# First pieces of x in 256 columns ahead of their weights, and square sums by a column of ones, in a hybrid decoder layer on one core

## The chip, the cores and the metric

The kernel runs on one core of one Trainium2 chip. The metric is the device time of one execution in microseconds (us); the median of several runs counts. The engines are TensorE (PE, with its weight loads as PEld), VectorE (DVE), ScalarE (ACT), GpSimd (POOL) and SyncE (SP), which here only issues loads and stores.

## What is computed

A decoder layer for 256 tokens of width 2048, all in float32. The input x is normed per row and goes through one combined projection to 12304 columns. Two mixers read its parts. Branch A is a gated DeltaNet with 8 heads of 128: queries, keys and values pass a causal convolution of four taps and a SiLU, and then a chunked delta rule. Branch B is a block attention with 8 heads of 128, which for 256 tokens is plain causal attention. Both are gated, projected, merged with sigmoid gates, projected once more, normed, and added to x. What matters for the change, cut from the reference:

```python
def l2_normalize(x):
    return x * lax.rsqrt(jnp.sum(x * x, axis=-1, keepdims=True) + NORM_EPS)
...
    h = rms_norm(x, pre_norm_w[l])
    proj = h @ w_in
...
    qkv = jax.nn.silu(causal_depthwise_conv(gdn_qkv, conv_w)).astype(jnp.float32)
    qa, ka, va = jnp.split(qkv, 3, axis=-1)
    qa, ka, va = l2_normalize(to_heads(qa)), l2_normalize(to_heads(ka)), to_heads(va)
```

So each head of the queries needs the sum of the squares of its 128 elements, per token.

## The kernel before, in words

**Products in parts.** Every large projection is done in two parts of float32r: an operand is cast to `hi` by ACT and the rest `lo` is the operand less `hi`, by DVE. A product is hi by hi, hi by lo and lo by hi, summed in PSUM. `split` (L220) does this for weights, in tiles of three buffers each, ahead of PE. Weights come through SP's queue into `raw`, by `proj_t` (L340), which has the weights stationary and gives channels by tokens, loading rows of 256 columns, and `proj_n` (L358), which has the activations stationary and gives tokens by channels, loading rows of 512 columns. `mm` (L146) and `tr` (L149) record matmuls and transposes, so PE's instructions have the line L147 or L150; both keep program order on PE.

**The start.** All loads of the start are issued by SP in the order of the code (L160 to L172): first the norm's weights `nrow`, then four times the pattern "512 columns of x, as two tiles of 128 tokens (L170), then four tiles of 128 rows by 512 columns of the keys' weights (L172)". PE waits with products of ones (`warm`), turns `nrow` into a column per 128 channels (`pnc`, L293; DVE copies it to `ncol`), and then turns x: `turn(c)` (L237) transposes the four tiles of 128 channels of one piece, eight transposes into `hTp`. `turned` (L248) writes the scaled result as hi (ACT, for k=1 DVE) and lo (DVE, L256) into `hT`. `first_split` (L274) casts the keys' weights (L278, L279), and `first_products` (L282) does the four heads' products of one k, eight instructions. The loop at L302 takes for each piece the products of its first two k, turns the next piece, takes the squares of x for the norm (`stats`), and then the products of its last two k. The reciprocal norm is applied later, since it is a factor per row.

**Ticks.** The work beside the projections hangs in queues of generators (`Queue`, L47). After every six or eight large products a `tick` lowers each queue's wait by 0.5; when it reaches zero the next part is put into the program there, and it says how long to wait for the part after. So PE's order is fixed by the code and by constants such as `SC_WAIT` and `A_WAIT1`. The order of the blocks of projections is the list `ORDER` (L42): queries 0 and 1 early, `kq2` and `kq3` (keys and queries of a pair of heads) later, the attention's `mk0` to `mk3` behind them, then gates and the branch pairs.

**Queries and scores.** `queries` projects two heads, convolves them and queues `score_pair` (L504). It writes hi and lo of keys and queries side by side into `kq` (ACT L509, DVE L510), and after `SC_WAIT` calls `scores` (L524) for each head. That makes two PSUM tiles `s1` and `s2` (both shown as `s`) of keys by keys and keys by queries, six products (L529), then two transposes of the queries' tile into the free half of `s2` (L532). DVE takes the diagonal of keys by keys for the keys' square sums (L534, L537). ACT squares the transposed queries and sums along the row, once for each 128 tokens (L542, `jq`), into `ssq`. `ssq` is used much later, in `normed` (L910). DVE scales the scores into `gdn` (L547, L555).

**Attention.** `attend` (L1031) waits `A_WAIT1`, does the scores `ms` of one head (L1034, L1035), the mask and the maximum on DVE, the exponentials on ACT; after `A_WAIT2` three transposes `pp`, after `A_WAIT3` the products `po` with the values, which DVE gates into `zm` (L1062). `turned_attention` (L1065) transposes `zm` (`pt`) after `A_WAIT4`. Two queues hold the heads of even and odd number. The keys `y_mk` of a pair are scaled by the row norm on DVE (L1084) before the scores. `branch_pair` (L832) empties these queues before its own products start. While the outputs of branch A are turned, `held` stops them.

Of the kernel before, what the change touches and what calls it, by code (L numbers as in the profile page):

```python
# [10 lines left out]
BF16 = mybir.dt.bfloat16  # L11
AF = mybir.ActivationFunctionType
# [3 lines left out]
P = 128  # L16
# [15 lines left out]
V_WAIT = 8  # L32
SV_WAIT = 1
OS_WAIT = 3
A_WAIT1 = 1.5
A_WAIT2 = 3
A_WAIT3 = 2
A_WAIT4 = 4
# [36 lines left out]
def hybrid_layer(  # L75
# [15 lines left out]
    nc = tc.nc  # L91
    B, S, D = x.shape
    NT = S // P
# [6 lines left out]
    xf = x.rearrange("b s d -> (b s) d")  # L100
# [15 lines left out]
    wk = ctx.enter_context(tc.tile_pool(name="wk", bufs=2))  # L116
# [7 lines left out]
    def acc_tile(name):  # L124
        return acc.tile([P, 512], F32, tag="acc", name=name)

    def aux_tile(name):
        return aux.tile([P, 512], F32, tag="aux", name=name)
# [17 lines left out]
    def mm(*args, **kwargs):  # L146
        return pin(nc.tensor.matmul(*args, **kwargs))  # L147

    def tr(*args):  # L149
        return pin(nc.tensor.transpose(*args))  # L150
# [8 lines left out]

    NCH = KT // 4  # L160
    nrow = cst.tile([KT, P], F32, name="nrow")
    nc.sync.dma_start(nrow, pre_norm_w.rearrange("o (k p) -> (o k) p", p=P))
    prow = big.tile([P, P], F32, tag="ga", name="prow")
    xall = big.tile([P, NT, D], F32, tag="u1", name="x")
    xs = [xall[:, t, :] for t in range(NT)]
    rawk = [big.tile([P, KT // 2, 512], F32, tag=f"g{i}", name=f"rawf_k{i}") for i in range(2)]
    for c in range(NCH):
        for t in range(NT):
            cs = slice(c * 512, (c + 1) * 512)
            nc.sync.dma_start(xs[t][:, cs], xf[t * P : (t + 1) * P, cs])  # L170
        for k in range(4 * c, 4 * c + 4):
            nc.sync.dma_start(rawk[k // 8][:, k % 8], w_in[k * P : (k + 1) * P, CK : CK + 512])  # L172


    ones = cst.tile([P, P], F32, name="ones")
    nc.vector.memset(ones, 1.0)
    ident = cst.tile([P, P], F32, name="ident")
# [56 lines left out]
    ssx = cst.tile([P, NT, 4], F32, name="ssx")  # L234
    pfirst = [acc_tile(f"a_k0_{m}") for m in range(4)]

    def turn(c):  # L237

        pts = []
        for k in range(4 * c, 4 * c + 4):  # L240
            if k % 2 == 0:
                pt = aux_tile(f"hTp_{k}")
            pts.append((k, pt[:, k % 2 * S : (k % 2 + 1) * S]))
            for t in range(NT):
                tr(pts[-1][1][:, t * P : (t + 1) * P], xs[t][:, k * P : (k + 1) * P], ident)
        return pts

    def turned(pts):  # L248
        for k, pr in pts:
            if k == 1:  # L250
                pin(nc.vector.tensor_scalar_mul(hT[:, k, :S], pr, ncol[:, k : k + 1]))
            else:
                pin(nc.scalar.activation(hT[:, k, :S], pr, AF.Copy, scale=ncol[:, k : k + 1]))
        for k, pr in pts:
            pin(
                nc.vector.scalar_tensor_tensor(  # L256
                    hT[:, k, S:], pr, ncol[:, k : k + 1], hT[:, k, :S].bitcast(F32), op0=ALU.mult, op1=ALU.subtract
                )
            )
# [14 lines left out]
    def first_split(k, n):  # L274
        hi = wspl.tile([P, 2, 512], F32R, tag="hi", name=f"hi_k0_{k}")
        lo = wspl.tile([P, 2, 512], F32R, tag="lo", name=f"lo_k0_{k}")
        raw = rawk[k // 8][:, k % 8 : k % 8 + n]
        pin(nc.scalar.copy(hi[:, :n], raw))  # L278
        pin(nc.vector.tensor_tensor(lo[:, :n], raw, hi[:, :n].bitcast(F32), op=ALU.subtract))  # L279
        return [(k + i, hi[:, i], lo[:, i]) for i in range(n)]  # L280

    def first_products(parts):  # L282
        for k, hi, lo in parts:
            for part in range(2):
                for m in range(4):
                    ms, pt = slice(m * P, (m + 1) * P), pfirst[m]
                    if part == 0:
                        mm(pt, hi[:, ms], hT[:, k, :], start=(k == 0), stop=False)
                    else:
                        mm(pt[:, :S], lo[:, ms], hT[:, k, :S], start=False, stop=(k == KT - 1))  # L290

    pnc = aux_tile("pnc")
    tr(pnc[:, :KT], nrow, ident[:KT, :KT])  # L293
    pin(nc.vector.tensor_copy(ncol, pnc[:, :KT]))
    pts = turn(0)
    for i in range(WARM2):
        mm(warm[:, :P], ones, ones, start=True, stop=True)
    turned(pts[:2])
    parts = first_split(0, 1) + first_split(1, 1)
    turned(pts[2:])  # L300
    parts += first_split(2, 2)
    for c in range(NCH):  # L302
        first_products(parts[4 * c : 4 * c + 2])
        if c + 1 < NCH:
            turned(turn(c + 1))
        if c == 0:
            parts += first_split(4, 2)
        stats(c)
        first_products(parts[4 * c + 2 : 4 * c + 4])
        for k in (4 * c + 6, 4 * c + 8):  # L310
            if k < KT:
                parts += first_split(k, 2)
# [174 lines left out]
    def sl(h):  # L487
        return gsl[h // HG][:, h % HG, :]
# [5 lines left out]
    ssk, ssq = nrm[:, 0], nrm[:, 1]  # L494
# [9 lines left out]
    def score_pair(h, kT, qT):  # L504
        kqs = []
        for m in range(2):
            kq = big.tile([P, 2, 2 * S], F32R, tag=("tt", "tw")[m], name=f"kq_{h + m}")
            for i, y in enumerate((kT[m], qT[m])):
                nc.scalar.copy(kq[:, i, :S], y)  # L509
                nc.vector.tensor_tensor(kq[:, i, S:], y, kq[:, i, :S].bitcast(F32), op=ALU.subtract)  # L510
            kqs.append(kq)
        yield SC_WAIT
        for m in range(2):
            yield from scores(h + m, kqs[m], qT[m])

        for b in range(4):
            t, p_ = b // 2, b % 2
            c0 = t * 4 * P + p_ * 64
            nc.gpsimd.dma_start(
                l_d[b, h : h + 2].rearrange("h j i -> j h i"),  # L520
                gsl[h // HG][p_ * 64 : p_ * 64 + 64, h % HG : h % HG + 2, c0 : c0 + 64],
            )

    def scores(h, kq, qT):  # L524
        p1 = aux_tile(f"s1_{h}")
        p2 = aux_tile(f"s2_{h}")
        for t, pt in enumerate((p1.rearrange("p (a n) -> p a n", a=2), p2[:, :S].rearrange("p (a n) -> p a n", a=2))):
            for i, (a, b) in enumerate(((0, 0), (0, S), (S, 0))):
                mm(pt, kq[:, 0, a + t * P : a + (t + 1) * P], kq[:, :, b + t * P : b + S], start=(i == 0), stop=(i == 2))  # L529
        yield 0.5  # L530
        for t in range(NT):
            tr(p2[:, (2 + t) * P : (3 + t) * P], qT[:, t * P : (t + 1) * P], ident)  # L532
        jk = wk.tile([P, P], BF16, tag="jk", name=f"jk_{h}")
        nc.vector.scalar_tensor_tensor(  # L534
            jk, p1[:, :P], 1.0, ident, op0=ALU.mult, op1=ALU.mult, accum_out=ssk[:, 0, h : h + 1]
        )
        nc.vector.scalar_tensor_tensor(  # L537
            jk, p2[:, :P], 1.0, ident, op0=ALU.mult, op1=ALU.mult, accum_out=ssk[:, 1, h : h + 1]
        )
        for t in range(NT):  # L540
            jq = wk.tile([P, P], BF16, tag="jq", name=f"jq_{h}_{t}")
            nc.scalar.activation(jq, p2[:, (2 + t) * P : (3 + t) * P], AF.Square, accum_out=ssq[:, t, h : h + 1])  # L542
        c_ = cj[:, :, h : h + 1]
        nc.vector.tensor_scalar_add(c_, ssk[:, :, h : h + 1], EPS)
        nc.vector.reciprocal(c_, c_)
        nc.vector.tensor_tensor(c_, c_, beta[:, :, h : h + 1], op=ALU.mult)
        nc.vector.scalar_tensor_tensor(  # L547
            sl(h)[:, 0 : 4 * P].rearrange("p (a n) -> p a n", a=2),
            p1.rearrange("p (a n) -> p a n", a=2),
            cj[:, 0, h : h + 1],  # L550
            dec[:, h, 0 : 2 * P].unsqueeze(1).to_broadcast([P, 2, 2 * P]),
            op0=ALU.mult,
            op1=ALU.mult,
        )
        nc.vector.scalar_tensor_tensor(  # L555
            sl(h)[:, 4 * P :].rearrange("p (a n) -> p a n", a=2),
            p2[:, : 2 * P].rearrange("p (a n) -> p a n", a=2),
            cj[:, 1, h : h + 1],
            dec[:, h, 2 * P :].unsqueeze(1).to_broadcast([P, 2, P]),
            op0=ALU.mult,  # L560
            op1=ALU.mult,
        )
        sc_left[0] -= 1
        if not sc_left[0]:
            nc.scalar.activation(sk, ssk, AF.Sqrt, bias=epst)
        yield 1
# [464 lines left out]
    def attend(h, qT, kT):  # L1031
        yield A_WAIT1
        ps = aux_tile(f"ms_{h}")
# [78 lines left out]
    for blk in ORDER:  # L1112
        n, c = blk[:2].rstrip("0123456789"), int(blk[-1])
# [126 lines left out]
    parts = []  # L1240
# [20 lines left out]
    c = 3  # L1261
    pts = [acc_tile(f"a_y{c}_{t}") for t in range(NT)]
# [43 lines left out]
```

## Time and profile before

| | us |
|---|---|
| median of three runs | 778.01 (776.86 to 778.92) |
| profiled execution | 777.05 |
| its span, first to last instruction | 775.4 |
| PE busy | 763.5 |
| DVE busy | 565.2 |
| ACT busy | 436.1 |
| POOL busy | 33.5 |

The profile is of one execution. A row of a timeline has its start in us from the span's start, its duration in us, the engine, the line, the operation, the tile written `<-` the tiles read, the shapes, and how many instructions are merged into the row (x8); in brackets stands how long the engine was idle before it and what ended that. Matmuls are pipelined: the durations of neighbours overlap, so what one costs is read from the distance of the starts. A float32 matmul shows as two instructions, a transpose or a float32r matmul as one. A row of a window has, behind its bounds and its length, the busy time and the count of each engine, the granted clock of TensorE (1.00 is full), the DMA share and GB/s. A row of waits has us in total, times, and the longest. A row of a tile has the shortest, median and longest duration in ns, and the first and last start. A row of loads has the count, the size of each, and the median us from issue to landing.

### The profile page before, as it was taken

How to read it: one execution, taken by the hardware profiler on the slowest of the kernel's cores; microseconds unless marked ns; L12 is line 12 of the kernel's file. 1: busy time of each engine (PE TensorE's matmuls, PEld its weight loads, DVE VectorE, ACT ScalarE, POOL GpSimd, SP SyncE). 2: the span in 40 equal slices, each digit the busy share in tenths (PEclk: the TensorE clock that was granted, in tenths of full speed). 3: DMA queues.
4: the chain of work that ended last, by engine and by line, in shares of the span. 5: the costliest groups of instructions: out<-in, count | busy, mean ns of one | idle time of the engine just before them, and what ended most of it. 6: DMA issues, size and time to landing. Idle time of an engine off the chain costs nothing.

```text
span 775.4 us, 10348 instructions
## 1 busy us (share of the span) xinstructions
PE 763.5 (98%) x3923; PEld 650.2 (84%) x3923; DVE 565.2 (73%) x914; ACT 436.1 (56%) x654; POOL 33.5 (4%) x61
## 2 busy tenths in 40 slices
PE   8999999999999999999999999999999999999995
PEld 7898988899888888888889888788888888888884
DVE  5777669885878898775547886686658776888853
ACT  5676666657655664454447475654455544556731
POOL 3000001112000000002001000000000000000000
PEclk9999999999999999999999999999999999999999
DMA  8576675457655556668336556657644956375912
GB/s 302 173 238 214 188 213 170 136 166 220 202 179 202 177 188 196 198 180 217 109 97 217 178 173 216 242 205 251 212 163 152 386 172 212 111 286 193 333 54 109
DMA packets 93656, 151.87 MB, mean 196 GB/s; under 512 B 3237, under 2 KB 46886, under 8 KB 93094
## 3 DMA queue, kind: packets, MB, share of 16 engines
q1 hardware_dynamic: 88902, 134.42, 53.4%
q0 software_dynamic: 4128, 15.74, 6.0%
q10 hardware_dynamic: 576, 1.05, 0.4%
q8 instruction: 31, 0.51, 0.3%
q14 instruction: 19, 0.16, 0.1%
HBM read 148.04 MB, written 3.15 MB: 195 GB/s over the span
## 4 chain that ended last, share of the span: by engine, by line
PE 95%; ACT 2%; DVE 2%; DMA 1%; SPq 0%; issue 0%; DVEq 0%
PE a_gb L147 11%; PE a_y L147 11%; PE a_ga L147 11%; PE a_zg L147 6%; PE a_mq L147 6%; PE a_v L147 6%; PE a_mk L147 6%; PE a_ub L147 6%; PE a_zm L147 6%; PE a_mv L147 5%; PE a_k L147 5%; PE a_ua L147 5%; PE a_q L147 4%; PE sv L147 2%; PE s L147 1%; DMA x<-in_x_dram 1%
## 5 line engine op out<-in xcount | busy, mean ns | idle before, releaser
L147 PE MATMUL a_ga<-hi_ga,hT 128*128 128x512 f32 x256 | 81.9, 393 | 0.0
L147 PE MATMUL a_gb<-hi_gb,hT 128*128 128x512 f32 x256 | 80.2, 390 | 0.0
L226 DVE TENSOR_TENSOR lo_gb<-raw_gb,hi_gb 128x1024 fp32r<-128x1024 f32 x32 | 38.9, 1223 | 25.1 <-ACT hi_gb L225 24.9
L147 PEld LDWEIGHTS a_gb<-hi_gb,hT 128*128 128x128 f32 x256 | 48.0, 188 | 10.6
L147 PEld LDWEIGHTS a_ga<-hi_ga,hT 128*128 128x128 f32 x256 | 48.1, 188 | 10.1
L225 ACT CAST hi_gb<-raw_gb 128x1024 fp32r<-128x1024 f32 x32 | 33.3, 1051 | 35.6 <-PE a_gb L147 26.5
L225 ACT CAST hi_ga<-raw_ga 128x1024 fp32r<-128x1024 f32 x32 | 33.7, 1055 | 34.0 <-PE a_ga L147 16.2
L226 DVE TENSOR_TENSOR lo_ga<-raw_ga,hi_ga 128x1024 fp32r<-128x1024 f32 x32 | 39.0, 1222 | 18.5 <-ACT hi_ga L225 18.3
L147 PE MATMUL a_ga<-lo_ga,hT 128*128 128x512 f32 x128 | 50.0, 391 | 0.1
L147 PE MATMUL a_gb<-lo_gb,hT 128*128 128x512 f32 x128 | 50.0, 391 | 0.0
L147 PE MATMUL a_zg<-hi_zg,hT 128*128 128x348 f32 (+1 forms) x192 | 47.0, 322 | 0.0
L147 PE MATMUL a_mq<-hT,hi_mq 128*128 128x512 f32 x128 | 46.8, 407 | 0.0
L147 PE MATMUL a_mk<-hT,hi_mk 128*128 128x512 f32 x128 | 46.1, 402 | 0.0
L147 PE MATMUL a_y<-hi_y,mT 128*128 128x512 f32 x144 | 46.1, 392 | 0.0
L147 PE MATMUL a_q<-hT,hi_q 128*128 128x512 f32 x128 | 46.0, 399 | 0.0
L147 PE MATMUL a_v<-hT,hi_v 128*128 128x512 f32 x128 | 45.3, 399 | 0.0
L147 PE MATMUL a_ub<-hi_ub,obT 128*128 128x512 f32 x128 | 41.3, 395 | 0.0
L147 PE MATMUL a_k<-hT,hi_k 128*128 128x512 f32 x128 | 40.6, 399 | 0.5 <-ACT hi_k L278 0.5
L147 PE MATMUL a_zm<-hi_zm,hT 128*128 128x512 f32 x128 | 40.5, 392 | 0.0
L147 PE MATMUL a_mv<-hi_mv,hT 128*128 128x512 f32 x128 | 40.1, 391 | 0.0
L147 PE MATMUL a_v<-hT,lo_v 128*128 128x256 f32 x128 | 35.9, 281 | 0.0
L147 PE MATMUL a_q<-hT,lo_q 128*128 128x256 f32 x128 | 35.9, 281 | 0.0
(377 smaller groups left out, 1972.8 us busy)
## 6 DMA issues: line engine op xcount, KB each, us to landing
raw_ga<-in_w_in_dram SPq DMA_DIRECT2D x16, 1024.0 KB, 5.1
raw_gb<-in_w_in_dram SPq DMA_DIRECT2D x16, 1024.0 KB, 5.7
raw_y<-in_w_out_dram SPq DMA_DIRECT2D x15, 1024.0 KB, 5.9
raw_q<-in_w_in_dram SPq DMA_DIRECT2D x8, 1024.0 KB, 5.6
raw_mv<-in_w_in_dram SPq DMA_DIRECT2D x8, 1024.0 KB, 5.1
raw_v<-in_w_in_dram SPq DMA_DIRECT2D x8, 1024.0 KB, 5.7
raw_zm<-in_w_in_dram SPq DMA_DIRECT2D x8, 1024.0 KB, 5.0
raw_mq<-in_w_in_dram SPq DMA_DIRECT2D x8, 1024.0 KB, 5.8
```

Of the source, the lines that this page charges most:

```text
L147: return pin(nc.tensor.matmul(*args, **kwargs))
L225: nc.scalar.copy(hi, raw)
L226: nc.vector.tensor_tensor(lo, raw, hi.bitcast(F32), op=ALU.subtract)
```

## The change

Four things. `nrow` is issued by ACT instead of SP. The first 512 columns of x come as four pieces, 256 columns by 128 tokens each, the first two ahead of the weights of k=0 and 1 and the next two ahead of those of k=2 and 3; `turn` takes a range of k, and k=0 is turned, split and multiplied before k=2 and 3 are turned. The queries' tile is squared in place by ACT, behind the last reader of the unsquared one, and in `scores` two products with one column of ones sum the squares over the 128 channels, in place of the two transposes; ACT copies the two columns to `ssq` in place of the two squares with sums. `A_WAIT1` goes from 1.5 to 2, which is one tick.

```diff
-A_WAIT1 = 1.5
+A_WAIT1 = 2
...
-    nc.sync.dma_start(nrow, pre_norm_w.rearrange("o (k p) -> (o k) p", p=P))
+    nc.scalar.dma_start(nrow, pre_norm_w.rearrange("o (k p) -> (o k) p", p=P))
...
-    for c in range(NCH):
-        for t in range(NT):
-            cs = slice(c * 512, (c + 1) * 512)
-            nc.sync.dma_start(xs[t][:, cs], xf[t * P : (t + 1) * P, cs])
-        for k in range(4 * c, 4 * c + 4):
+
+    def load_x(c0, c1):
+        for t in range(NT):
+            nc.sync.dma_start(xs[t][:, c0:c1], xf[t * P : (t + 1) * P, c0:c1])
+
+    def load_k(k0, k1):
+        for k in range(k0, k1):
             nc.sync.dma_start(rawk[k // 8][:, k % 8], w_in[k * P : (k + 1) * P, CK : CK + 512])
+
+    for c in range(2):
+        load_x(c * 256, (c + 1) * 256)
+        load_k(2 * c, 2 * c + 2)
+    for c in range(1, NCH):
+        load_x(c * 512, (c + 1) * 512)
+        load_k(4 * c, 4 * c + 4)
...
-    def turn(c):
+    def turn(k0, k1):
...
-        for k in range(4 * c, 4 * c + 4):
+        for k in range(k0, k1):
...
-    pts = turn(0)
+    pts = turn(0, 2)
     for i in range(WARM2):
         mm(warm[:, :P], ones, ones, start=True, stop=True)
-    turned(pts[:2])
+    turned(pts)
     parts = first_split(0, 1) + first_split(1, 1)
-    turned(pts[2:])
+    first_products(parts[:1])
+    turned(turn(2, 4))
     parts += first_split(2, 2)
     for c in range(NCH):
-        first_products(parts[4 * c : 4 * c + 2])
+        first_products(parts[max(1, 4 * c) : 4 * c + 2])
         if c + 1 < NCH:
-            turned(turn(c + 1))
+            turned(turn(4 * c + 4, 4 * c + 8))
...
             kqs.append(kq)
+
+            nc.scalar.activation(qT[m], qT[m], AF.Square)
         yield SC_WAIT
...
         for t in range(NT):
-            tr(p2[:, (2 + t) * P : (3 + t) * P], qT[:, t * P : (t + 1) * P], ident)
+            mm(p2[:, 2 * P + t : 2 * P + t + 1], qT[:, t * P : (t + 1) * P], ones[:, 0:1], start=True, stop=True)
...
-        for t in range(NT):
-            jq = wk.tile([P, P], BF16, tag="jq", name=f"jq_{h}_{t}")
-            nc.scalar.activation(jq, p2[:, (2 + t) * P : (3 + t) * P], AF.Square, accum_out=ssq[:, t, h : h + 1])
+        nc.scalar.copy(ssq[:, :, h : h + 1], p2[:, 2 * P : 2 * P + NT].unsqueeze(2))
```

## The prediction

> **What bounds the kernel now.** I read the busy times first, then what TensorE (PE) waited for, then the chain of work that ended last over the first 36 us.
>
> ```profile
> PE 763.5 (98%) x3923; PEld 650.2 (84%) x3923; DVE 565.2 (73%) x914; ACT 436.1 (56%) x654; POOL 33.5 (4%) x61
> ```
> ```profile
> PE hTp L150 <- DMA x<-in_x_dram: 1.5, 2, 0.9
> PE warm L147 <- DVE epst L181: 1.1, 1, 1.1
> PE ms L147 <- DVE y_mk L1084: 0.7, 1, 0.7
> PE a_k L147 <- ACT hi_k L278: 0.5, 1, 0.5
> ```
>
> PE is busy for 98% of the span, and the second fence is its whole list of waits: us in total, times, longest. Three belong to the first 9 us. One, 0.7 us for `y_mk`, lies in the attention. Otherwise PE has its next operand when it wants it. So every us of PE work that an edit adds or removes after the start is a us of the end, and ScalarE (ACT) and VectorE (DVE) have room.
>
> The chain tells what bounds the start:
>
> ```profile
> 0.81 0.39 SPq L162
> ...
> 1.25 0.41 SPq L170
> ...
> 4.08 0.45 SPq L170
> ...
> 4.57 6.89 DMA x<-in_x_dram
> ```
> ```profile
> 9.00:12.00 3.00, 2.87 (x20) 2.35 (x19) 2.59 (x5) 1.05 (x1) 0.00 (x0) 1.00 1.03 356
> ```
> ```profile
> 3.98 0.28 PE L150 MATMUL pnc<-ident,nrow 16*128 16x16 f32 x1
> ...
> 6.11 0.98 PE L150 MATMUL hTp<-ident,x 128*128 128x128 f32 x7 [0.88 <-DMA x<-in_x_dram]
> ...
> 8.23 1.17 PE L147 MATMUL a_k<-hT,hi_k 128*128 128x512 f32 x4 [0.46 <-ACT hi_k L278]
> ...
> 11.10 1.38 PE L150 MATMUL hTp<-ident,x 128*128 128x128 f32 x8
> ```
>
> SP issues the loads one behind the other (L162 is `nrow`, L170 is x). The chain does not go through the first product at 8.23 us. It goes from the issues through a transfer of 6.89 us that lands at 11.46: the second half of the second 512 columns of x. PE has done the products of k=0 and 1 by then, began the next eight transposes at 11.10, and stood before the second of them. From there the chain goes on with PE. In the window 9 to 12 us the DMA share is 1.03 at 356 GB/s, so that landing comes as early as the bytes ahead of it allow.
>
> **The change, part by part.**
>
> *The start.* `nrow` leaves SP's queue, so the first x load is issued at 0.81 in place of 1.25: 0.44 us earlier. The first 512 columns of x become four pieces of 128 KB in place of two of 256 KB, the first two ahead of two weight tiles, so k=0 can begin earlier, by something between the 0.44 and about 1.1 us (0.44, and half of x's first two tiles no longer ahead of the weights: 256 KB at 356 GB/s is 0.7). But ahead of the landing at 11.46 lie the same bytes as before, `nrow`'s 8 KB apart. PE will do k=0, the four transposes of k=2 and 3 (4 x 0.11 us, below), k=1, and then stand before the same x tile, only longer. So the start gains what that landing gains: 0.44 us, less the price of shorter rows, 1 KB in place of 2 KB. Loads with either row show it:
>
> ```profile
> raw_q<-in_w_in_dram SPq DMA_DIRECT2D x8, 1024.0 KB, 5.6
> ...
> raw_zm<-in_w_in_dram SPq DMA_DIRECT2D x8, 1024.0 KB, 5.0
> ```
>
> `raw_q` has 1 KB rows and `raw_zm` 2 KB rows; 0.6 us on 1 MB, so at most 0.3 us on these 512 KB, and nothing if those 0.6 us come from other load. I take 0.2: **a gain of 0.25 us**. Bounds: a gain of 1.1 (the landing no longer binds and PE's earlier start counts whole), and a loss of 0.5 (SP has one issue more ahead of that tile, at some 0.45 us each, two pieces added for `nrow` taken away, and the landing might follow the issue). I keep near the middle, since the share of 1.03 says that bytes bind. After it PE has the same work as before, and DVE and ACT the same instructions in another order.
>
> *The square sums.* Per head two transposes go and two f32 products with one moving column come, eight heads, on PE at 108 to 177 us. What one costs is read from when the next instruction starts, not from its own duration, since they overlap. First f32 products with 16 and 8 columns, the only ones so narrow with 128 x 128 weights:
>
> ```profile
> 60.82 0.39 PE L147 MATMUL a_q<-hT,hi_q 128*128 128x512 f32 x1
> 61.05 0.28 PE L147 MATMUL a_q<-hT,lo_q 128*128 128x256 f32 x1
> 61.17 0.29 PE L147 MATMUL pg<-sp,tri_u 128*128 128x16 f32 x2
> 61.31 0.37 PE L147 MATMUL pg<-sp,ones 128*128 128x8 f32 x2
> 61.53 0.48 PE L147 MATMUL a_mv<-hi_mv,hT 128*128 128x512 f32 x1
> 61.85 0.39 PE L147 MATMUL a_mv<-lo_mv,hT 128*128 128x512 f32 x1
> ```
> ```profile
> 114.04 0.28 PE L147 MATMUL a_k<-hT,lo_k 128*128 128x256 f32 x1
> 114.15 0.38 PE L150 MATMUL s<-ident,y_q 128*128 128x128 f32 x2
> 114.29 0.48 PE L147 MATMUL a_k<-hT,hi_k 128*128 128x512 f32 x1
> 114.61 0.28 PE L147 MATMUL a_k<-hT,lo_k 128*128 128x256 f32 x1
> ```
>
> A 512-column product takes 0.23 (60.82 to 61.05), a 256-column one 0.12 (61.05 to 61.17). Without `pg`, the product behind `a_mv<-hi_mv` would have started at 61.05 + 0.12 + 0.23 = 61.40; it started at 61.85. So two f32 products, which are four instructions (x2 and x2), cost 0.45 us, 0.11 for each. In the second fence: 114.04 + 0.12 + 0.23 = 114.39 without transposes, 114.61 with them: two transposes, two instructions, cost 0.22, again 0.11 each. An f32 product is two weight loads and a transpose one, and 16 moving columns cost no less than 128. So a head goes from 0.22 to 0.45, and eight heads are **a loss of 8 x 0.23 = 1.84 us**. No row shows one column: between free (a gain of 8 x 0.22 = 1.76) and the 0.45 of these rows, I take the 0.45, the nearest row, since cost did not fall from 128 columns to 8.
>
> ACT loses sixteen squares from PSUM with their accumulator reads, gains eight squares over 256 columns in place and eight tiny copies. The new square waits for DVE's subtraction that reads the same `qT`, and behind it in ACT's queue stand the casts of the weights, for which PE would wait. What hides it:
>
> ```profile
> ACT jq L542 <- DVE jk L537: 5.1, 4, 1.8
> ```
> ```profile
> L475 ACT ACTIVATE y_q<-y_q x8: 407/418/421, 67.1 to 170.1; 128x256 f32<-128x256 f32 x8
> ```
>
> ACT already stands up to 1.8 us for DVE at the square that goes, and PE's list shows no wait for it. A square of 0.42 us (the SiLU of the same tile), needed only some ticks later, fits: nothing. If that cover were gone, each of eight would cost up to 0.42, 3.4 us in all.
>
> *A_WAIT1 from 1.5 to 2.* The scores of the attention come one tick later (six 512-column products, 1.37 us). The place of PE's wait:
>
> ```profile
> 439.51 0.82 PE L147 MATMUL ms<-y_mk,y_mq 128*128 128x128 f32 x4
> ...
> 441.57 0.59 PE L147 MATMUL a_ga<-hi_ga,hT 128*128 128x512 f32 x1
> ```
> ```profile
> 411.23 1.48 PE L147 MATMUL ms<-y_mk,y_mq 128*128 128x128 f32 x8
> 412.36 0.58 PE L147 MATMUL a_mq<-hT,hi_mq 128*128 128x512 f32 x1
> ```
>
> The eight instructions take 2.06 us to the next product where one head's `y_mk` is late, 1.13 where it isn't. The lateness is 0.93, less than the tick of 1.37: **a gain of 0.9 us**. Late next is what hangs behind those scores, one tick later too:
>
> ```profile
> 482.86 1.12 DVE L1062 SCALAR_TENSOR_TENSOR zm<-po,sm,zm 128x128 f32<-128x128 f32 x4
> ...
> 484.11 1.22 DVE L226 TENSOR_TENSOR lo_ua0p<-raw_ua,hi_ua0p 128x1024 fp32r<-128x1024 f32 x1
> ...
> 485.57 0.60 PE L150 MATMUL pt<-ident,zm 128*128 128x128 f32 x4
> ```
>
> `zm` would end at 482.86 + 1.12 + 1.37 = 485.35, just ahead of `pt`, which keeps its place before the branch pair. If `lo_ua0p` gets in front of it, it ends at 484.11 + 1.22 + 1.12 = 486.45 and PE stands for 0.9. I count nothing for it; the bounds of this edit are a gain of 0.9 and nothing.
>
> **Sum**: -0.25 + 1.84 - 0.9 = +0.7 us. The profiled execution took 777.05 (its span of 775.4 and 1.65 around it), so 777.75; it lay 0.96 below the median of the three runs. On the median, 778.01 + 0.7 = **778.7 us**: 0.1% more, within 0.3% (2.3 us), about what a measurement of this kernel can tell from no change.
>
> **The rivals.**
>
> *One column is nearly free.* If a pass of one column went at the pace of issue, with its weight load hidden behind the product before, the exchange would give back up to 1.76 us: -0.25 - 1.76 - 0.9 = -2.9, 775.1 us, faster. Against it stands that 8, 16 and 128 columns all step at 0.11 us; for it, that no row shows one column. The Trainium skill's page "TensorE: Matmul & The Clock Gate", section "Back-to-back issue gap", gives about 60 cycles (25 ns) for 1 to 64 columns. By that the 32 passes would be 0.8 us, the exchange a gain of 0.96 and the sum -2.1, 775.9 (an estimate from that page). The rows of `pg` speak against that figure, at 0.11 where it says 0.025. 8%.
>
> *`nrow` comes late on ACT's queue*, the one that ends slower.
>
> ```profile
> 0.80 1.28 ACT L182 ACT_TABLE_LOAD   x1 [0.80 <-PEq L1292]
> 2.09 0.19 ACT L182 COPY rstd<-epst 128x2 f32<-128x2 f32 x1
> ```
> ```profile
> rawf_k<-in_w_in_dram SPq DMA_DIRECT2D x16, 256.0 KB, 5.4
> ...
> nrow<-in_pre_norm_w_dram SPq DMA_DIRECT2D x1, 8.0 KB, 1.5
> ```
>
> If the issue comes behind table load and copy, at 2.28 + 0.4, and lands like the loads issued then (5.4) and not as it did on idle engines (1.5), it is there at 8.1. `pnc` stands ahead of all transposes on PE. With its 0.28, the 2.12 from transposes to first product (6.11 to 8.23), the 2.87 to the next transposes (to 11.10) and 0.45 for the moved ones, PE comes to its next x tile at 13.8, 2.3 behind 11.5: 2.3 + 1.84 - 0.9 = +3.2, 781.3 us. It decides from a landing at about 5.5 us. Against it: the issue is ACT's first instruction in program order, as it is SP's now, and has no wait. 7%.
>
> *PE's earlier start counts whole*: the start gains 1.1, sum -0.2, 777.8. The DMA share of 1.03 speaks against. 11%.
>
> *The later scores gain nothing*, since `pt` stands for the 0.9 that `ms` no longer does: sum +1.6, 779.6. 11%, of which 2 go past 0.3% with other stalls.
>
> **How the numbers follow.** The forecast has 60%, the rivals 8, 7, 11 and 11, and 3 stay for a stall that I don't see (the casts behind the new square, +3.4), slower. Faster: 8%. Within 0.3%: 60 + 11 + 9 = 80%. Slower: 7 + 3 + 2 = 12%. The range leaves out the free column and late `nrow`. It goes from 777.8, and from 779.6, by the about 1 us that single runs lie from their median: 776.5 to 780.6.
>
> **What would show it.** Start: the first product clearly before 8.2 us, but PE's wait for x ahead of k=4 longer than now and ended near 11.2. Square sums: 32 instructions of one column with about 0.11 us to the next start, PE's instructions up by 16, and no wait of PE for ACT near 70 to 180 us. Scores: no wait for `y_mk`; if `pt` or `lo_ga` near 485 us waits instead, the fourth rival holds. Wrong altogether if the one-column products step at well under 0.1 us, if `pnc` moves past 5.5 us, or if casts run late behind the new square.

## The result, and the profile after

The changed kernel takes 780.41 us (median of six executions, 779.01 to 780.87), the kernel before 777.95 (six, 776.86 to 778.92): a ratio of 1.0031, 95% interval 1.0019 to 1.0043. That is 2.46 us slower where +0.7 was forecast. The difference is 0.31%, about the 0.3% that the prediction takes as the least that a measurement can tell from no change, and the interval reaches to both sides of it. The profiled execution took 780.39 us, its span 778.7.

TensorE's busy time in the kernel after, from the page:

```profile
PE 766.3 (98%) x3939; PEld 653.1 (84%) x3939; DVE 565.8 (73%) x914; ACT 435.1 (56%) x638; POOL 33.8 (4%) x61
```

PE has 16 instructions more (3939 against 3923) and is busy 2.8 us longer; it is still the bound. All its waits in the kernel after:

```profile
PE hTp L150 <- DMA x<-in_x_dram: 1.5, 2, 1.1
PE warm L147 <- DVE epst L191: 1.1, 1, 1.1
PE a_k L147 <- DVE hT L266: 0.9, 1, 0.9
PE a_v L147 <- DVE lo_v L236: 0.8, 1, 0.8
PE a_v L147 <- ACT hi_v L235: 0.3, 1, 0.3
```

The wait of `ms` for `y_mk` is gone. Two are new, both of a product `a_v` of the values' projection for one late weight tile, 1.1 us together. No part of the change touches the values.

To see where the time goes, cut the span at three PE instructions that every version has: the first `pg` (behind the start), the first `a_ga` (behind queries and values), and the last product. The `pg` row of before, 61.17, stands in the prediction. The other two in the kernel before, and all three in the kernel after:

```profile
215.00 0.48 PE L147 MATMUL a_ga<-hi_ga,hT 128*128 128x512 f32 x1
...
767.13 0.40 PE L147 MATMUL a_y<-hi_y,mT 128*128 128x512 f32 x1
```
```profile
61.95 0.29 PE L147 MATMUL pg<-sp,tri_u 128*128 128x16 f32 x2
...
219.10 0.48 PE L147 MATMUL a_ga<-hi_ga,hT 128*128 128x512 f32 x1
...
770.57 0.40 PE L147 MATMUL a_y<-hi_y,mT 128*128 128x512 f32 x1
```

The start ends 0.78 later (61.95 - 61.17), the middle takes 157.15 in place of 153.83 (+3.32), the rest 551.47 in place of 552.13 (-0.66). Together +3.44 in these two executions.

**The middle.** First the columns, in the kernel after:

```profile
109.30 0.28 PE L147 MATMUL a_q<-hT,lo_q 128*128 128x256 f32 x1
109.42 0.50 PE L147 MATMUL s<-ones,y_q 128*128 128x1 f32 x4
109.78 0.47 PE L147 MATMUL a_q<-hT,hi_q 128*128 128x512 f32 x1
110.09 0.28 PE L147 MATMUL a_q<-hT,lo_q 128*128 128x256 f32 x1
```

From the `lo_q` ahead to the `lo_q` behind are 0.79 us. A product of 256 and one of 512 columns take 0.35 of it, so the four one-column instructions cost 0.44, 0.11 each: what 128, 16 and 8 columns cost before. They replace two transposes of 0.22, and eight heads make 8 x 0.22 = 1.8, the loss that the prediction has.

The rest of the 3.32 lies near 195 us. PE in the kernel after:

```profile
194.32 0.28 PE L147 MATMUL a_v<-hT,lo_v 128*128 128x256 f32 x1
194.44 0.40 PE L147 MATMUL a_v<-hT,hi_v 128*128 128x512 f32 x1
194.68 0.28 PE L147 MATMUL a_v<-hT,lo_v 128*128 128x256 f32 x1
195.23 0.50 PE L147 MATMUL a_v<-hT,hi_v 128*128 128x512 f32 x1 [0.27 <-ACT hi_v L235]
196.49 0.38 PE L147 MATMUL a_v<-hT,lo_v 128*128 128x256 f32 x1 [0.76 <-DVE lo_v L236]
```

Two `lo_v` in a row are 0.36 apart (194.32 to 194.68), and then 1.81 (to 196.49): 1.45 us lost. What was late is told by ACT's rows, first of the kernel before, then of the kernel after:

```profile
186.67 1.05 ACT L225 CAST hi_v<-raw_v 128x1024 fp32r<-128x1024 f32 x1 [1.22 <-PE a_v L147]
189.06 3.17 ACT L646 COPY lc<-lc 32x1024 f32<-32x1024 f32 x3 [1.34 <-DMA lc<-l_d]
...
192.52 1.05 ACT L225 CAST hi_v<-raw_v 128x1024 fp32r<-128x1024 f32 x1
```
```profile
185.31 2.19 ACT L235 CAST hi_v<-raw_v 128x1024 fp32r<-128x1024 f32 x2
190.94 3.16 ACT L657 COPY lc<-lc 32x1024 f32<-32x1024 f32 x3 [3.44 <-DMA lc<-l_d]
194.12 1.05 ACT L235 CAST hi_v<-raw_v 128x1024 fp32r<-128x1024 f32 x1
```

Before, a cast of `hi_v` comes at 186.67 and the three copies of `lc` behind it. After, the copies come ahead of that cast. They wait 3.44 us for a load, hold ACT until 194.10, and the cast runs from 194.12 to 195.17. DVE's `lo_v` of that tile starts at 195.21. So ACT, with 44% of the span idle, has stood before a load with a cast behind it that PE wanted. In the code the copies are kept in program order (`pin`), the casts of `split` are not, and the edit leaves both where they were in the code. So their order on ACT was chosen when the kernel was compiled, and it is not given by the code alone.

**The rest of the span** has the scores on time, in the kernel after:

```profile
445.26 1.47 PE L147 MATMUL ms<-y_mk,y_mq 128*128 128x128 f32 x8
446.38 0.58 PE L147 MATMUL a_ga<-hi_ga,hT 128*128 128x512 f32 x1
```

From `ms` to the next product are 1.12, before 2.06. Nothing new waits behind.

**The start** in the kernel after:

```profile
3.98 0.28 PE L150 MATMUL pnc<-ident,nrow 16*128 16x16 f32 x1
4.19 1.04 PE L150 MATMUL hTp<-ident,x 128*128 128x128 f32 x4
5.07 0.83 PE L147 MATMUL warm<-ones 128*128 128x128 f32 x6
6.80 1.17 PE L147 MATMUL a_k<-hT,hi_k 128*128 128x512 f32 x4 [0.90 <-DVE hT L266]
...
11.55 0.33 PE L150 MATMUL hTp<-ident,x 128*128 128x128 f32 x1 [1.12 <-DMA x<-in_x_dram]
12.26 0.98 PE L150 MATMUL hTp<-ident,x 128*128 128x128 f32 x7 [0.37 <-DMA x<-in_x_dram]
```

The first product comes at 6.80 in place of 8.23, `nrow` is not late (`pnc` at 3.98 as before), and PE stands before the x tile of k=4, as forecast. But it goes on at 12.26, 0.8 later than the landing at 11.46 before.

### The profile page after: what moved, and what is told of

Its sections match the earlier page's. It is cut to its first block, busy times and chain, and to the rows that moved or that the text cites. A ratio compares the mean times of both kernels' runs of the same rounds, so it can differ in the third digit from the quotient of the medians.

```text
span 778.7 us, 10361 instructions
## 1 busy us (share of the span) xinstructions
PE 766.3 (98%) x3939; PEld 653.1 (84%) x3939; DVE 565.8 (73%) x914; ACT 435.1 (56%) x638; POOL 33.8 (4%) x61
## 4 chain that ended last, share of the span: by engine, by line
PE 93%; ACT 2%; DMA 2%; DVE 1%; issue 1%; SPq 0%; POOL 0%; DVEq 0%; POOLq 0%
PE a_gb L147 11%; PE a_ga L147 11%; PE a_y L147 11%; PE a_mq L147 6%; PE a_mk L147 6%; PE a_ub L147 6%; PE a_zm L147 6%; PE a_k L147 5%; PE a_zg L147 5%; PE a_mv L147 5%; PE a_ua L147 5%; PE a_q L147 4%; PE a_v L147 4%; PE sv L147 2%; PE s L147 1%; DMA x<-in_x_dram 1%
## 5 line engine op out<-in xcount | busy, mean ns | idle before, releaser
L147 PE MATMUL a_mq<-hT,lo_mq 128*128 128x256 f32 x128 | 36.0, 281 | 0.0
```

## The experiments

All versions compute the same thing. The diffs here are cut to the lines that mark an edit; the rest of each part is in the diff of the change. "Before" was measured again beside each set: medians 778.00 for the first four, 777.92 for the next four, 777.87 for the last two. Each edit is against the kernel before, if not said otherwise.

**One part alone: the columns.**

```diff
+            nc.scalar.activation(qT[m], qT[m], AF.Square)
...
-            tr(p2[:, (2 + t) * P : (3 + t) * P], qT[:, t * P : (t + 1) * P], ident)
+            mm(p2[:, 2 * P + t : 2 * P + t + 1], qT[:, t * P : (t + 1) * P], ones[:, 0:1], start=True, stop=True)
...
```

> The kernel before with the column sums alone (squares in place, products with a column of ones, small copies); loads and A_WAIT1 as before. Theory: two parts add, 1.8 us of PE work (16 more weight loads at 0.11) and some 1.5 us because ACT's order at the second block of values changes, three copies of lc that wait for a transfer now standing ahead of a cast of the values' weights; so +2.4 us (the second part gone, +0.9 wait not gained) to +3.4, and PE waiting for hi_v and lo_v. Rival: the wait at the values comes from the later start or from A_WAIT1, and this kernel is at +1.8 with no such wait.

Measured: 781.55, ratio 1.0050 (1.0038 to 1.0063), +3.55. PE's list of waits in this version holds the two of `a_v` (0.8 and 0.4), and on ACT the three copies of `lc` start at 191.36, ahead of the cast at 194.54: the columns alone turn ACT's order around.

**One part alone: the start.**

```diff
...
+    for c in range(2):
+        load_x(c * 256, (c + 1) * 256)
+        load_k(2 * c, 2 * c + 2)
...
```

> The kernel before with the start alone (nrow on ACT's queue, four pieces of x of 256 columns, first k by itself); columns and A_WAIT1 as before. Theory: first product near 6.8 us, but the x tile of k=4 lands no earlier than before, +0.3 to +0.8 us. Rival: the late landing of 12.2 us in the changed kernel was chance of that execution, and the start gains 0.25, with that tile at 11.2.

Measured: 776.83, ratio 0.9986 (0.9978 to 0.9995), -1.17. Neither expectation holds: the theory had a loss, the rival a gain of 0.25.

**One part alone: the wait.**

```diff
-A_WAIT1 = 1.5
+A_WAIT1 = 2
```

> The kernel before with A_WAIT1 at 2 alone. Theory: PE's wait for y_mk of 0.9 us goes and nothing takes its place, -0.9 us. Rival: another wait comes near 485 us, where the last transposes of zm stand, and the time does not change.

Measured: 777.14, ratio 0.9993 (0.9984 to 1.0002), -0.86, about the -0.9 expected, with an interval that reaches just past no change.

**The columns with ACT's old order.** The copies of `lc` are put three ticks later, which brings the cast ahead of them again (and a second cast ahead of the last copy).

```diff
-LC_WAIT = 3.5
+LC_WAIT = 5
```

> The column sums alone, with the wait ahead of the copies of lc at 5 instead of 3.5, so that they stand behind the cast of the values' weights in ACT's order again; PE's instructions are those of the kernel with the column sums alone. Theory: no wait of PE at the values, 1.5 us less than that kernel, +1.8 against before. Rival: the wait at the values is made by something else, such as the load of the weights, and stays.

Measured: 779.71, ratio 1.0022 (1.0012 to 1.0032), +1.71. About half of the loss of the columns is gone, and what stays agrees with the 1.84 of the prediction. The kernel before with `LC_WAIT` at 5 alone was not run. ACT in this version, and all that PE waits for:

```profile
189.98 1.05 ACT L225 CAST hi_v<-raw_v 128x1024 fp32r<-128x1024 f32 x1 [1.72 <-PE a_v L147]
191.81 2.10 ACT L645 COPY lc<-lc 32x1024 f32<-32x1024 f32 x2 [0.78 <-DMA lc<-l_d]
193.94 1.05 ACT L225 CAST hi_v<-raw_v 128x1024 fp32r<-128x1024 f32 x1
```
```profile
PE hTp L150 <- DMA x<-in_x_dram: 1.4, 2, 0.7
PE warm L147 <- DVE epst L181: 1.1, 1, 1.1
PE ms L147 <- DVE y_mk L1083: 0.7, 1, 0.7
```

**Why does the start gain more than its load?** The version with the wait alone has the old start, and its profile shows another pace there than the profile of before did:

```profile
4.82 0.47 PE L150 MATMUL hTp<-ident,x 128*128 128x128 f32 x1 [0.56 <-DMA x<-in_x_dram]
6.13 1.75 PE L150 MATMUL hTp<-ident,x 128*128 128x128 f32 x7 [0.84 <-DMA x<-in_x_dram]
7.68 1.49 PE L147 MATMUL warm<-ones 128*128 128x128 f32 x6
8.82 2.05 PE L147 MATMUL a_k<-hT,hi_k 128*128 128x512 f32 x4
10.67 1.05 PE L147 MATMUL a_k<-hT,lo_k 128*128 128x256 f32 x4
11.53 1.18 PE L147 MATMUL a_k<-hT,hi_k 128*128 128x512 f32 x4
...
13.01 1.04 PE L150 MATMUL hTp<-ident,x 128*128 128x128 f32 x8
```

Seven transposes take 1.75 where before shows 0.98, and four products of 512 columns step by 1.85 in all (8.82 to 10.67), about twice the later pace. PE comes to its next transposes at 13.01, not 11.10, and doesn't wait there for the x tile of k=4, which has landed. The theory: TensorE is at half pace until it has been busy long enough, the old start leaves it idle ahead of and between x tiles (0.56 and 0.84 us here), and the new one closes these gaps. Rival: the gain is x that lands earlier. More products of ones ahead of the old start touch the first alone:

```diff
-WARM = 6
+WARM = 12
```

> The kernel before with twelve products of ones ahead of the first transposes in place of six, so that PE has no gap of 1.2 us between the first and the second tile of x; nothing else. Theory: in three of four profiles with the old start PE ran its first products at half pace until 10.6 to 12.0 us (distance of 512-column products 0.43 in place of 0.23), and the gain of the new start is mostly that its PE is at full pace from 5.3; so more ones give the same: full pace by 8 us, the next transposes near 11.5, and 0.7 to 1.3 us less than before. Rival: the gain of the new start comes from the earlier x, and more ones change nothing or cost up to 0.4 since the transposes come behind them.

Measured: 777.11, ratio 0.9985 (0.9977 to 0.9994), -0.81, with the loads as they were: most of the gain, as the theory has it. The profile shows the first products at full pace. What TensorE has to do to count as busy was not tested apart: more ones fill the gaps, and they are also more work of one kind.

**The whole change with `LC_WAIT` at 5.**

> The changed kernel with the wait ahead of the copies of lc at 5 instead of 3.5. Theory: the single edits add: +1.7 for the columns without the wait at the values, -1.2 for the start, -0.9 for the scores, -0.3 against before and some 1.8 under the changed kernel. Rival: the changed kernel has a start of its own that is 0.7 us later (x tile of k=4 at 12.2 in its profile, 11.5 in that of the start alone), and this one is at +0.5.

Measured: 777.89, ratio 1.0003 (0.9994 to 1.0012), -0.03, between the -0.3 of the theory and the +0.5 of the rival, and its interval, -0.5 to +0.9, holds both. Against the change as it was, it is 2.5 us less. The order of the casts and copies on ACT accounts for 1.5 of it (157.15 - 155.61 in the middle stretch, in the table below); in these two profiles the start differs too, by 1.15 (61.95 against 60.80), with the same instructions.

**The whole change without the columns** (start and wait).

> The changed kernel without its column sums: the start and A_WAIT1 at 2, with the two transposes and the squares from PSUM. Theory: -1.2 - 0.9 = -2.0 us against before, and no wait at y_mk or at the values. Rival: the gains overlap or the start gives 0.25 alone, -1.2.

Measured: 776.59, ratio 0.9978 (0.9969 to 0.9987), -1.33: faster than both kernels. The sum of the two single gains, -2.0, was expected, and -1.2 if they don't add; the interval, -2.4 to -1.0, holds both. PE's waits in it:

```profile
PE warm L147 <- DVE epst L191: 1.1, 1, 1.1
PE a_k L147 <- ACT hi_k L288: 0.8, 1, 0.8
PE hTp L150 <- DMA x<-in_x_dram: 0.7, 1, 0.7
```

**On top of that, the products of k=2 ahead of the transposes of k=4,** so that PE works while that x tile lands.

```diff
-    parts += first_split(2, 2)
+    parts += first_split(2, 1) + first_split(3, 1)
...
-        first_products(parts[max(1, 4 * c) : 4 * c + 2])
+        mid = 3 if c == 0 else 4 * c + 2
+        first_products(parts[max(1, 4 * c) : mid])
...
-        first_products(parts[4 * c + 2 : 4 * c + 4])
+        first_products(parts[mid : 4 * c + 4])
```

> The one without column sums, with the products of k=2 moved ahead of the transposes of k=4 to 7, and k=2 and 3 cast one by one: the work that PE has when it waits for that x tile. Theory: PE's wait of 0.7 to 1.7 us for the tile goes, 0.8 us less than the one without column sums, -2.8 against before. Rival: the casts of k=2 come so late (its weights land near 9 us) that PE waits for them as long, no difference.

Measured: 776.99, ratio 0.9989 (0.9980 to 0.9998), -0.93: no gain over 776.59, where 0.8 was expected. The rival holds. PE's waits:

```profile
PE a_k L147 <- ACT hi_k L288: 1.5, 2, 0.8
PE warm L147 <- DVE epst L191: 1.1, 1, 1.1
```

The wait for x is gone, and a second one for the casts of the weights has taken its place, with the same sum (1.5 against 0.8 + 0.7).

**Ones and wait, without the new loads.** `WARM` at 12 and `A_WAIT1` at 2.

> The kernel before with WARM at 12 and A_WAIT1 at 2, loads of the start untouched. If the start's gain is TensorE's clock being up when the first products come, ones alone replace the new order of loads and this run stands where start and wait together stood: -0.81 - 0.86 = -1.7 against before, about 776.3, and its first products step at 0.23 us for 512 columns. If the new order of loads brings something of its own (x earlier), this run stays behind start and wait together (776.6) by the 0.3 to 0.4 by which start alone led the ones alone, at 776.9 or later.

Measured: 776.66, ratio 0.9984 (0.9975 to 0.9993), -1.21. That lies between the 776.3 of the theory and the 776.9 of the other case, and is as fast as start and wait together (776.59): no run shows that the new loads bring anything that six more ones don't bring.

**Start, wait and more ones.**

> Start and wait together with WARM at 12. If the clock is already up by the first products with the new loads, more ones bring nothing (776.6, within 0.4) as long as they end before x lands. If the new loads only bring it up in some executions, ones bring a further gain of up to 0.5, 776.1. If the ones are in front of the first transposes, up to 6 x 0.06 = 0.4 later, 777.0.

Measured: 776.96, ratio 0.9987 (0.9978 to 0.9996), -0.91. No further gain; with the ones ahead, `pnc` starts at 6.35 in place of 3.98, so the six cost 2.4 us at that place and not 0.4, and the time comes out at the 777.0 of the third case.

The three stretches of the span in every profile, cut as above (us; first `pg`, from there to the first `a_ga`, from there to the last product):

| | start | middle | rest |
|---|---|---|---|
| before | 61.17 | 153.83 | 552.13 |
| after | 61.95 | 157.15 | 551.47 |
| columns alone | 62.20 | 157.32 | 552.08 |
| start alone | 61.19 | 153.60 | 552.12 |
| wait alone | 62.71 | 153.42 | 551.53 |
| columns, `LC_WAIT` 5 | 62.73 | 155.58 | 552.10 |
| more ones | 61.56 | 153.54 | 552.06 |
| change, `LC_WAIT` 5 | 60.80 | 155.61 | 551.37 |
| change without columns | 60.92 | 153.83 | 551.55 |
| and k=2 first | 61.70 | 153.61 | 551.43 |
| ones and wait | 61.69 | 153.80 | 551.58 |
| start, wait, ones | 61.95 | 153.86 | 551.54 |

The middle falls into three groups: 153.4 to 153.9 without columns (mean 153.69), 155.6 with columns and ACT's old order, 157.15 and 157.32 with columns and the new order. The rest falls into two, 552.1 and 551.5, by `A_WAIT1`. The start scatters from one execution to the next.

## Where the prediction was right and where it was wrong, point by point

**The columns on PE: right.** +1.84 was forecast; the middle shows 155.60 - 153.69 = +1.9, and the run with ACT's old order +1.71. Sixteen columns, eight and one all cost 0.11 us per instruction, and each instruction has a weight load of its own (PEld counts 3939 as PE does). The rival of the free column is false.

By the table of the Trainium skill's "Back-to-back issue gap" (page "TensorE: Matmul & The Clock Gate"), about 25 ns for so few columns, the exchange would have been a gain; the section says itself that this gap leaves the weight loads out. The trace has 110 ns, and the measurement decides. The same page's section "LDWEIGHTS (loading the stationary operand)" gives a weight load by its columns, P / 1.2, which for 128 is 107 ns; the 110 ns of the trace agree. That the weight load sets them was not tested apart.

**The columns on ACT: wrong, and the step that failed.** The prediction put it: "A square of 0.42 us (the SiLU of the same tile), needed only some ticks later, fits: nothing." It does fit where it stands, with no wait of PE for ACT from 70 to 180 us; the stall that was feared there, casts behind the new square, didn't come. What it cost came at 195 us: the edit altered ACT's load, the compiled order of ACT's queue changed, and three copies that wait for a load went ahead of a cast. Price: 157.24 - 155.60 = 1.6 in the middle (means of the two with and the two without the new order), 1.45 read from the PE rows; by the medians 781.55 - 779.71 = 1.8 and 780.41 - 777.89 = 2.5. The two runs that move nothing but the copies of `lc` show it, and every kernel without the columns has the old order. The medians of the second pair hold more than the stall, since their starts differ. Why the compiler chose so was not looked into.

**`A_WAIT1`: right in kind, somewhat too large.** -0.9 forecast. The wait itself gave back 0.94 (2.06 to 1.12); the rest of the span shows -0.60, and the time -0.86 with an interval that reaches from -1.2 to +0.2. The 0.3 between is lost ahead of that wait, in the block of the attention's queries and keys, where the scores of the earlier heads come one tick later too: from the first `a_mq` to the last `a_mk` it takes 120.12 to 120.13 us in the five profiles with `A_WAIT1` at 1.5 and 120.37 to 120.47 in the seven with 2. Which instructions lose it was not followed. The rival that `pt` stands for it instead is false.

**The start: right sign, mis-sized, and for another reason.** -0.25 forecast, from a landing of x that comes earlier. PE went on with the x of k=4 at 12.26 in the kernel after, at 11.57, 11.13 and 11.22 in the three other profiles with this order and no added ones; 11.46 was the landing before. So the landing scatters by more than the forecast gain, and the prediction's premise that it comes as early as the bytes ahead of it allow gives no time to within 0.25 us. What did gain is the pace: the four profiles with the old start and its six ones end it at 61.17, 62.20, 62.71 and 62.73 (mean 62.20), the four with the new one and no further edit of the start at 61.95, 61.19, 60.80 and 60.92 (mean 61.22), -1.0; alone it measured -1.17. The profile of before was the one of four that had full pace early, and the prediction read its start as the rule. "PE's earlier start counts whole" had about the right gain, for a reason that it didn't name, which is luck. `nrow` late on ACT's queue is false.

**The sum.** With the measured terms: -1.0 + 1.9 + 1.6 - 0.6 = +1.9; measured +2.46, its interval reaching from +1.5 to +3.3. The forecast missed a loss of 1.6 and 0.7 of a gain at the start, and had 0.3 too much of a gain for the wait. The errors partly cancelled, and that the range held the time (780.41, its end at 780.6) was luck. The prediction gave 3% to a stall that it didn't see and named casts behind the new square for it, at +3.4; the stall that came is another, at half that price. Whether the half us between 1.9 and 2.46 is anything more than scatter stays open, as does whether the new order of loads is worth anything beside the ones: -1.17 and -0.81 don't differ by more than their intervals.

## What to carry to other kernels

An edit that adds or removes instructions on an engine can change that engine's compiled order far away from the edit: compare the engine's order before and after, and look for an instruction that waits for a load with one behind it that the bound engine wants. A part that looks free on a half-idle engine is only free in that order. Where a kernel's start is at stake, read it from several profiles, since one execution may show the better of two paces.

## What the runs showed of the hardware

TensorE's pace at the start is a matter of chance from one execution to the next, and of how steadily it is busy. With the old start three of four profiles ran the first products at half pace: 1.85 us for four of 512 columns in the version with the wait alone. None of the eight with the new start or with more ones did: 1.00 in the change without columns, here:

```profile
6.88 1.16 PE L147 MATMUL a_k<-hT,hi_k 128*128 128x512 f32 x4 [0.85 <-ACT hi_k L288]
7.88 0.71 PE L147 MATMUL a_k<-hT,lo_k 128*128 128x256 f32 x4
```

The trace's record of the granted clock turns to full at 4.7 to 7.0 us in these and in the profile of before, and at 10.2, 11.7 and 11.7 in the other three; from there to the turn back after the last product it lasts 768.0, 764.6 or 761.2 us, which are steps of 3.41. The Trainium skill's page "TensorE: Matmul & The Clock Gate", section "What's actually happening", says that the clock stands at half until TensorE was busy for a window of about 3.4 us, that these windows run free of the kernel, and that the point of change so differs between runs. The traces agree, in the step of 3.41 and in the factor of two. The same section gives the scatter of that point as half a us to each side; here, with gaps between the x tiles, four profiles with the same old start have it at 4.7, 10.2, 11.7 and 11.7 us, and the measurement decides.

The column of the granted clock doesn't show this. The window of 8 to 10 us in the version with the wait alone, in the midst of the half pace:

```profile
8.00:10.00 2.00, 2.00 (x9) 1.81 (x9) 2.00 (x6) 2.00 (x5) 0.47 (x1) 1.00 1.02 333
```

It says 1.00, since the record has no entry ahead of the first change. The pace is read from the distance of the starts.
